# Two thirds of the gate projections by seven block products, in a stage of their own behind the attention

## The chip, the cores and the metric

The kernel runs on one core of a Trainium2 chip. The core has five engines with a queue of instructions each, worked off in order: TensorE (PE, matmuls), VectorE (DVE), ScalarE (ACT), GpSimd (POOL) and SyncE (SP), which here issues nearly all DMA transfers. The metric is the device time of one execution in microseconds (us), as the median of several runs.

## What is computed

One step of a hybrid encoder layer for 1152 tokens of width 1024, all in float32. The part that matters here is the gated merge of three branches:

```python
h = rmsnorm(x, p['g_pre1'])
y_ssm = y_ssm * jax.nn.sigmoid(y_ssm @ p['w_glu'] + p['b_glu'])
gates = jax.nn.sigmoid(h @ p['w_gate'] + p['b_gate']).reshape(bsz, L, N_BRANCH, D_MODEL)
merged = (gates[:, :, 0] * (y_ssm @ p['w_br_ssm'])
          + gates[:, :, 1] * (y_pool @ p['w_br_pool'])
          + gates[:, :, 2] * (y_mem @ p['w_br_mem']))
```

`w_gate` is 1024 x 3072: 24 blocks of 128 output columns, called gates 0 to 23 here (0 to 7 for the state-space branch, 8 to 15 for the pooling branch, 16 to 23 for the memory attention). Around the merge stand a state-space scan, a pooling branch, a small cross-attention, an output projection and a conv FFN, which the change leaves as they are.

## The kernel before, in words

Activations lie transposed: 128 features on the partitions, tokens along the row, in three chunks of 384 tokens. PE multiplies in a reduced float32 format (fp32r), so every operand is split into a high and a low part (`split`: ACT copies the high part, DVE subtracts to get the low one), and one product of a 128-row block is three matmuls, high x high, low x high, high x low (`mm3`, lines 101 to 107; the order prints the low part of h as hlo, of the weights as wlo). A gate of one chunk has 8 k-blocks, so 24 matmuls of 128x384, then DVE multiplies by the row norms (`scaled`, line 200), ACT takes the sigmoid (line 930), and the result, 192 KB, goes to a branch or is stored in the DRAM buffer `Dsg`.

The program runs through phase1 (norm, input projection, scan, attention, some gates), phase_g (branches and merge), phase_o (output projection), and the FFN. A scheduler orders each engine's instructions ahead of time; products without other ties are used as filler between the steps of the scan and the attention.

- **phase1** (line 864) puts 14 gates, 8 to 15 and 0 to 5, for all three chunks into `Dsg`, as filler beside scan and attention. The attention of the prompt (`attention`, lines 836 to 861) runs over two halves g and two head pairs hp; in each half a head's scores are four matmuls of 128x512, ACT takes the exponential, two matmuls sum over the memory (line 855), DVE takes a RECIPROCAL of 64x512 from PSUM and multiplies (lines 856, 857), and the result is stored to `Dmem` (line 858). Behind the first half stand the second part of the decode attention (64 matmuls of 128x32, line 769, that read four loads `cv`) and of the pooling branch.
- **phase_g** (line 992) loads the branch operands from `Dmem` and `Dpool` (`load_pair`, line 941; tile br), splits them (ohi, olo), and goes over f = 0 to 7 and the chunks. `branch` (line 979) computes gate 16 + f inline, 24 matmuls, beside 6 matmuls of the memory branch, then 6 of the pooling branch, whose gate is loaded from `Dsg` (tile sgl, 192 KB). Then `glu` (line 965) makes 48 matmuls a chunk, with a gate (number 6) between the chunks, and the last loop has the state-space branch, 12 matmuls per f and chunk, with gates from `Dsg` but the last (number 7), computed inline.

Apart from its weights a gate product in phase_g reads only SBUF: h stays there as hhi and hlo in all chunks.

## Time and profile before

| | us |
|---|---|
| median of 3 runs (lowest to highest) | 1556.09 (1555.48 to 1556.93) |
| profiled execution: its own time | 1553.49 |
| its span, first to last instruction | 1551.6 |
| PE busy | 1535.3 (99%) |
| DVE busy | 1018.7 (66%) |
| ACT busy | 583.5 (38%) |
| POOL busy | 442.1 (28%) |

The page's tables and the answers of the trace share a form: line of the code, engine, operation, output <- inputs, shape, count; then busy time in us, mean of one in ns, and the idle time before them with what ended it. In a timeline row the first number is the start and the second the duration; brackets hold the idle time before it and its releaser. Rows of a window give, for each engine, busy us and (x instructions), then the granted clock of PE (1.00 is full), the DMA share and GB/s. A row of waits gives the total, the number and the longest. Rows of transfers give the count, the size, and the median us from issue to landing. Neighbouring matmuls overlap in the records: their durations are longer than their distance.

### The profile page before, as it was taken

How to read it: one execution, taken by the hardware profiler on the slowest of the kernel's cores; microseconds unless marked ns; L12 is line 12 of the kernel's file. 1: busy time of each engine (PE TensorE's matmuls, PEld its weight loads, DVE VectorE, ACT ScalarE, POOL GpSimd, SP SyncE). 2: the span in 40 equal slices, each digit the busy share in tenths (PEclk: the TensorE clock that was granted, in tenths of full speed). 3: DMA queues.
4: the chain of work that ended last, by engine and by line, in shares of the span. 5: the costliest groups of instructions: out<-in, count | busy, mean ns of one | idle time of the engine just before them, and what ended most of it. 6: DMA issues, size and time to landing. Idle time of an engine off the chain costs nothing.

```text
span 1551.6 us, 22930 instructions
## 1 busy us (share of the span) xinstructions
PE 1535.3 (99%) x9016; PEld 1502.2 (97%) x9016; DVE 1018.7 (66%) x1606; ACT 583.5 (38%) x895; POOL 442.1 (28%) x425
## 2 busy tenths in 40 slices
PE   9999999999999999999999999999999999999997
PEld 8999998888999999999999999999999999999997
DVE  7956987556633354637587665665566569888876
ACT  8313445344311241435454333333343343333322
POOL 0000010000121243300025344344344311565545
PEclk9999999999999999999999999999999999999998
DMA  7533334422522235123413112212221243222224
GB/s 270 170 103 103 110 115 165 135 93 82 168 77 72 74 92 160 54 89 115 152 38 131 72 56 86 72 64 78 72 79 63 72 141 131 75 102 97 91 73 168
DMA packets 98029, 161.34 MB, mean 104 GB/s; under 512 B 23169, under 2 KB 68609, under 8 KB 97921
## 3 DMA queue, kind: packets, MB, share of 16 engines
q1 hardware_dynamic: 97488, 159.65, 31.4%
q8 instruction: 70, 1.15, 0.3%
q14 instruction: 39, 0.31, 0.1%
q10 hardware_dynamic: 432, 0.23, 0.1%
HBM read 117.43 MB, written 42.42 MB: 103 GB/s over the span
## 4 chain that ended last, share of the span: by engine, by line
PE 88%; DVE 6%; DMA 2%; ACT 2%; issue 1%; SPq 0%; POOL 0%; DVEq 0%; ACTq 0%; POOLq 0%
PE pc L107 16%; PE pc L103 16%; PE pc L106 16%; PE ps L103 11%; PE ps L106 11%; PE ps L107 11%; DMA Ts<-DG 1%; PE ps L855 1%; DMA DG<-gs 1%; ACT hhi L126 1%; DVE mg L1131 1%; PE ps L1078 0%; PE ps L769 0%; PE ps L821 0%; DVE Xs L604 0%
## 5 line engine op out<-in xcount | busy, mean ns | idle before, releaser
L103 PE MATMUL pc<-hhi,whi 128*128 128x384 f32 x760 | 257.1, 338 | 0.0
L107 PE MATMUL pc<-hhi,wlo 128*128 128x384 f32 x760 | 255.8, 337 | 0.3 <-DVE wlo L64 0.3
L106 PE MATMUL pc<-hlo,whi 128*128 128x384 f32 x760 | 256.1, 337 | 0.0
L63 ACT ACTIVATE whi<-rawt 128x1024 fp32r<-128x1024 f32 (+1 forms) x99 | 103.5, 1047 | 186.3 <-PE pc L106 78.3
L64 DVE TENSOR_TENSOR wlo<-rawt,whi 128x1024 fp32r<-128x1024 f32 (+1 forms) x99 | 122.5, 1239 | 54.6 <-ACT whi L63 54.2
L103 PEld LDWEIGHTS pc<-hhi,whi 128*128 128x128 f32 x760 | 142.7, 188 | 2.6 <-issue 1.1
L107 PEld LDWEIGHTS pc<-hhi,wlo 128*128 128x128 f32 x760 | 142.7, 188 | 2.3 <-issue 0.7
L106 PEld LDWEIGHTS pc<-hlo,whi 128*128 128x128 f32 x760 | 142.7, 188 | 2.0 <-issue 0.5
L200 DVE TENSOR_TENSOR sg<-pc,rb 128x384 f32<-128x384 f32 x95 | 52.3, 553 | 114.2 <-PE pc L107 112.8
L107 PE MATMUL pc<-h2hi,wlo 128*128 128x384 f32 x352 | 118.9, 338 | 0.0
L106 PE MATMUL pc<-h2lo,whi 128*128 128x384 f32 x352 | 118.3, 336 | 0.5 <-DVE h2lo L64 0.5
L103 PE MATMUL pc<-h2hi,whi 128*128 128x384 f32 x352 | 118.3, 336 | 0.0
L63 ACT ACTIVATE S<-S 128x512 fp32r<-128x512 f32 x80 | 50.2, 630 | 140.7 <-PE ps L107 86.9
L64 DVE TENSOR_TENSOR S<-S,S 128x512 fp32r<-128x512 f32 x80 | 68.7, 861 | 46.2 <-ACT S L63 44.2
L930 ACT ACTIVATE sg<-sg,vec 128x384 f32<-128x384 f32 x72 | 44.1, 612 | 141.4 <-DVE sg L200 112.8
L103 PE MATMUL ps<-bT,S 128*128 128x384 f32 x240 | 80.2, 334 | 0.0
L107 PE MATMUL ps<-bT,S 128*128 128x384 f32 x240 | 80.2, 334 | 0.0
L106 PE MATMUL ps<-bT,S 128*128 128x384 f32 x240 | 80.2, 334 | 0.0
L1017 POOL TENSOR_TENSOR mg<-mg,sgl 128x384 f32<-128x384 f32 x24 | 29.1, 1213 | 165.4 <-DVE sgl L1015 162.0
L63 ACT ACTIVATE dhi<-dwr 128x1024 fp32r<-128x1024 f32 x38 | 39.6, 1057 | 84.4 <-PE pc L106 49.2
L106 PEld LDWEIGHTS pc<-h2lo,whi 128*128 128x128 f32 x352 | 66.0, 187 | 0.8 <-DVE h2lo L64 0.8
L107 PEld LDWEIGHTS pc<-h2hi,wlo 128*128 128x128 f32 x352 | 66.1, 188 | 0.0
(449 smaller groups left out, 4225.9 us busy)
## 6 DMA issues: line engine op xcount, KB each, us to landing
rawt<-in_w_up SPq DMA_DIRECT2D x44, 512.0 KB, 3.4
Dact<-t SPq DMA_DIRECT2D x22, 576.0 KB, 3.6
rawt<-in_w_gate SPq DMA_DIRECT2D x24, 512.0 KB, 3.6
dwr<-in_w_down SPq DMA_DIRECT2D x22, 512.0 KB, 3.4
Dsg<-sg SPq DMA_DIRECT2D x45, 192.0 KB, 1.8
sgl<-Dsg SPq DMA_DIRECT2D x45, 192.0 KB, 2.4
dBr<-Dact SPq DMA_DIRECT2D x8, 768.0 KB, 5.0
xT<-in_xT SPq DMA_DIRECT2D x12, 384.0 KB, 7.6
```

Of the source, the lines that this page charges most:

```text
L63: a = nc.scalar.activation(hi, src, AF.Copy)
L64: return a, (eng or nc.vector).tensor_sub(lo, src, hi)
L103: i = nc.tensor.matmul(out, whi, xhi, start=start, stop=False)
L106: nc.tensor.matmul(out, whi, xlo, start=False, stop=False)
L107: nc.tensor.matmul(out, wlo, xhi, start=False, stop=stop)
L126: a = nc.scalar.activation(hi[:, k, :], x[:, k, :], AF.Copy, scale=g)
L200: self.nc.vector.tensor_mul(sg, b, self.rb[:, c, :])
L855: nc.tensor.matmul(o, va[:, m, 2 * hp + e, :], pT[:, m, :], start=m == 0, stop=m == 1)
L930: self.nc.scalar.activation(sg, sg, AF.Sigmoid, bias=self.vec[:, V_BGATE + m:V_BGATE + m + 1])
L1017: nc.gpsimd.tensor_add(m, m, sp)
L1131: V.scalar_tensor_tensor(oT[:, f, :], oT[:, f, :], self.vec[:, V_GPRE2 + f:V_GPRE2 + f + 1], rb, op0=OP.mult, op1=OP.mult)
```

## The change

Gates 8 to 15 stay in phase1 for all chunks. Gates 16 to 23 and 0 to 7 are taken in 8 pairs of neighbours. For chunk 2 each is computed as before, in phase1. For chunks 0 and 1 a pair is a 2 x 2 block product: two gates' weights, each in two halves of k (a11, a12, a21, a22), times two chunks of h, each in two halves of k (b11, b21, b12, b22). It is computed by seven products of sums of blocks, each with 4 k-blocks (12 matmuls), where there were eight (the form of Strassen's scheme due to Winograd).

- `blocks` loads xT of chunks 0 and 1 once more (8 transfers of 384 KB, issued behind the first store of the attention, `att_half`), scales them to h on DVE (16 instructions of 128x384, line 964 of the new file), and forms the sums with 5 subtractions of 128x1536 and 7 splits of 128x1536 (tiles bB11, bB21, bB22, bT1 to bT4).
- Still in phase1, the two products with a11 and a12 (on bB11 and bB21) use the split weights of the even gate that chunk 2 uses. Their sum is the even gate of chunk 0; the first is kept (tile u).
- `phase_s`, a new stage between phase1 and phase_g, loads the raw weights of a pair again (2 x 512 KB), forms four sums on DVE (128x512), splits five operands, runs five products in the order 6, 5, 7, 3, 4, and adds the results on DVE, POOL and ACT into the other three gates of the pair, which are stored to `Dsg`.
- `branch` no longer computes a gate: all 24 come from `Dsg`, the pool of the loaded gates has 6 buffers for 3, and the gate between the glu chunks is gone.

```diff
-        self.Dsg = D.tile([9 + NSG, 3, 128, 384], F32, name="Dsg")
+        self.Dsg = D.tile([24, 3, 128, 384], F32, name="Dsg")
...
+            for m in range(8, 16):
+                gates(m, range(3))
+            self.blocks()
+
+            for m in self.strassen_gates()[1::2]:
+                gates(m, (2,))
+            self.su = []
+            for m in self.strassen_gates()[0::2]:
+                gw = gates(m, (2,))
+                self.su.append(su.tile([128, 384], F32, tag="su", name="u"))
+                for n, ks in (("B11", slice(0, 4)), ("B21", slice(4, 8))):
+                    b = self.block(self.pc(), [w[:, ks] for w in gw], n)
...
+    def blocks(self):
+        V = self.nc.vector
+        lo, up = slice(0, 4), slice(4, 8)
+        with self.tc.issue_after(self.att_half.ins):
+            h = [self.h_load(c) for c in range(2)]
+        for c in range(2):
+            for k in range(8):
+                V.scalar_tensor_tensor(h[c][:, k, :], h[c][:, k, :], self.vec[:, V_GPRE1 + k:V_GPRE1 + k + 1],
+                                       self.rb[:, c, :], op0=OP.mult, op1=OP.mult)
...
+        op("B11", h0[:, lo])
+        op("B21", h0[:, up])
...
+                V.tensor_add(s1, a21, a22)
+                V.tensor_sub(s2, s1, a11)
...
+            nxt = weights(0)
+            for j in range(8):
+                cur, nxt = nxt, weights(j + 1) if j < 7 else None
+                for p in (6, 5, 7, 3, 4):
+                    prod(cur, p)
...
-        if gw is None:
-            sg = self.load_gate(P, 8 + f, c)
-        else:
-            sg = self.gate(P, 8 * g + f, self.proj(gw, c, 8, *self.hx()), c)
+        sg = self.load_gate(P, 8 * g + f, c)
...
-            for c in range(3):
-                os.append(self.glu(P, w, c))
-                nc.sync.dma_start(self.Dsg[8 + NSG, c], self.gate(P, NSG, self.proj(gw, c, 8, *self.hx()), c))
-            os = self.opx(os)
+            os = self.opx([self.glu(P, w, c) for c in range(3)])
...
+        k.phase_s()
+        k.rbs.close()
         k.phase_g()
```

Up to the attention the engines' orders are the same. Three places behind that are shown. The first is DVE's order in the attention of the prompt, from the third of eight reciprocals; yt is the attention's output, wlo a gate weight's low part. Before:

```order
574 L856 RECIPROCAL yt<-ps 64x512
575 L857 TENSOR_TENSOR yt<-ps,yt 64x512
576 L200 TENSOR_TENSOR sg<-pc,rb 128x384
577 L64 TENSOR_TENSOR wlo<-rawt,whi 128x1024
578 L856 RECIPROCAL yt<-ps 64x512
579 L857 TENSOR_TENSOR yt<-ps,yt 64x512
580 L200 TENSOR_TENSOR sg<-pc,rb 128x384
```

And of the changed kernel, from the same reciprocal to the low part of B21 (bB_3484 is B11, bB_3487 is B21):

```order
580 L855 RECIPROCAL yt<-ps 64x512
581 L964 SCALAR_TENSOR_TENSOR xT<-xT,vec,rb 128x384 x3
582 L199 TENSOR_TENSOR sg<-pc,rb 128x384
583 L964 SCALAR_TENSOR_TENSOR xT<-xT,vec,rb 128x384 x3
584 L856 TENSOR_TENSOR yt<-ps,yt 64x512
585 L964 SCALAR_TENSOR_TENSOR xT<-xT,vec,rb 128x384 x4
586 L855 RECIPROCAL yt<-ps 64x512
587 L964 SCALAR_TENSOR_TENSOR xT<-xT,vec,rb 128x384 x4
588 L63 TENSOR_TENSOR bB_3484<-xT,bB_3484 128x1536
589 L964 SCALAR_TENSOR_TENSOR xT<-xT,vec,rb 128x384 x2
590 L63 TENSOR_TENSOR bB_3487<-xT,bB_3487 128x1536
```

Fourteen of the sixteen scalings and a second reciprocal now stand between the third reciprocal and the low part of B11. PE's order at the same place, from the fourth head's sums (at) over the decode attention (PT, cv) on. Before:

```order
1727 L855 MATMUL ps<-at_2255 128x512
1728 L769 MATMUL ps<-PT,cv 128x32 x2
1729 L855 MATMUL ps<-at_2255 128x512
1730 L769 MATMUL ps<-PT,cv 128x32 x14
1731 L107 MATMUL pc<-hhi,wlo 128x384
1732 L103 MATMUL pc<-hhi,whi 128x384
```

And of the changed kernel:

```order
1724 L854 MATMUL ps<-at_2258 128x512
1725 L768 MATMUL ps<-PT,cv 128x32 x8
1726 L854 MATMUL ps<-at_2258 128x512
1727 L768 MATMUL ps<-PT,cv 128x32 x8
1728 L102 MATMUL pc<-bB_3484,whi 128x384
1729 L768 MATMUL ps<-PT,cv 128x32 x16
1730 L105 MATMUL pc<-bB_3484,whi 128x384
1731 L106 MATMUL pc<-bB_3484,wlo 128x384
```

Where a gate on hhi stood, the first product on B11 stands now. The second place is the beginning of phase_g on PE. Before, the first branch product (ohi, olo) is mixed with a gate (hhi, hlo):

```order
2041 L103 MATMUL ps<-ohi,whi 128x384
2042 L103 MATMUL pc<-hhi,whi 128x384
2043 L106 MATMUL pc<-hlo,whi 128x384
2044 L107 MATMUL pc<-hhi,wlo 128x384
2045 L103 MATMUL pc<-hhi,whi 128x384
2046 L106 MATMUL pc<-hlo,whi 128x384
2047 L107 MATMUL pc<-hhi,wlo 128x384
2048 L106 MATMUL ps<-olo,whi 128x384
```

And of the changed kernel, from the last block product (bT4) on; ohi_5223 and ohi_5227 are the first memory operand, ohi_5233 belongs to the first pooling operand:

```order
L106 MATMUL pc_5185<-bT4_3507,A22_5033 128x384
L102 MATMUL ps_5286<-ohi_5223,whi_5217 128x384
L105 MATMUL ps_5286<-olo_5224,whi_5217 128x384
L106 MATMUL ps_5286<-ohi_5223,wlo_5218 128x384
L102 MATMUL ps_5286<-ohi_5227,whi_5217 128x384
L102 MATMUL ps_5294<-ohi_5233,whi_5217 128x384
L105 MATMUL ps_5286<-olo_5228,whi_5217 128x384
L106 MATMUL ps_5286<-ohi_5227,wlo_5218 128x384
```

Only branch products follow the last block product. SP's transfers there, before, with the last store of the attention (yt), the last store of a gate (sg), branch operands (br) and loaded gates (sgl):

```order
L858 DMA Dmem_84<-yt_2674 128x4x128
L925 DMA Dsg_98<-sg_4009 128x384
L941 DMA br_4063<-Dmem_84 128x2x384
L935 DMA sgl_4149<-Dsg_98 128x384
L935 DMA sgl_4196<-Dsg_98 128x384
L935 DMA sgl_4243<-Dsg_98 128x384
L941 DMA br_4073<-Dpool_85 128x2x384
L941 DMA br_4083<-Dmem_84 128x2x384
L941 DMA br_4093<-Dpool_85 128x2x384
```

And of the changed kernel, where x of phase_o comes in ahead, and the last gate's store is sg_5198:

```order
L1039 DMA Dsg_98<-sg_5181 128x384
L1230 DMA x_7015<-in_xT 128x768
L1230 DMA x_7039<-in_xT 128x768
L1073 DMA sgl_5284<-Dsg_98 128x384
L1039 DMA Dsg_98<-sg_5198 128x384
L1073 DMA sgl_5301<-Dsg_98 128x384
L1073 DMA sgl_5305<-Dsg_98 128x384
L1073 DMA sgl_5322<-Dsg_98 128x384
L1073 DMA sgl_5326<-Dsg_98 128x384
L1073 DMA sgl_5343<-Dsg_98 128x384
L1079 DMA br_5251<-Dpool_85 128x2x384
L1079 DMA br_5261<-Dmem_84 128x2x384
```

The load of br_5271 follows; three loaded gates stood ahead of the last three operands before, six now, and two loads of x. The third place is glu on PE, from the end of chunk 0's last product (pc_5402 before, pc_5908 now). Before, the gate (hhi_155) follows:

```order
L103 MATMUL pc_5402<-ohi_5332,whi_5302 128x384
L106 MATMUL pc_5402<-olo_5333,whi_5302 128x384
L107 MATMUL pc_5402<-ohi_5332,wlo_5303 128x384
L103 MATMUL pc_5424<-hhi_155,whi_5308 128x384
L106 MATMUL pc_5424<-hlo_156,whi_5308 128x384
```

Now chunk 1's first operand (ohi_5935) is read at once:

```order
L102 MATMUL pc_5908<-ohi_5838,whi_5814 128x384
L105 MATMUL pc_5908<-olo_5839,whi_5814 128x384
L106 MATMUL pc_5908<-ohi_5838,wlo_5815 128x384
L102 MATMUL pc_5956<-ohi_5935,whi_5808 128x384
L102 MATMUL pc_5978<-ohi_5935,whi_5808 128x384
```

More of the change, by code (lines that the diff above doesn't have):

```diff
@@ L19 @@
 EPS = 1e-6
-NSG = 6
 V_GPRE1, V_GPRE2, V_GMEM, V_BGATE, V_BGLU = 0, 8, 16, 24, 48
@@ L857, in attention @@
                     nc.vector.tensor_mul(yf[es], o[es], yf[es])
-                nc.sync.dma_start(self.Dmem[hp].rearrange("p (j k) -> p j k", j=8)[:, gs, 0:128], yt)
+                i = nc.sync.dma_start(self.Dmem[hp].rearrange("p (j k) -> p j k", j=8)[:, gs, 0:128], yt)
+                if g == hp == 0:
+                    self.att_half = i
             if g == 0:
@@ L917, in phase1, with gates @@
             nc.sync.dma_start(self.O["pool"], self.pout)
-            for f in range(8 + NSG):
-                m = 8 + f if f < 8 else f - 8
+            def gates(m, chunks):
                 with tc.high_priority():
                     gw = self.load_w(self.I["w_gate"][m])
-                for c in range(3):
+                for c in chunks:
                     b = self.proj(gw, c, 8, *self.hx())
                     with tc.high_priority():
-                        nc.sync.dma_start(self.Dsg[f, c], self.gate(P, m, b, c))
+                        nc.sync.dma_start(self.Dsg[m, c], self.gate(P, m, b, c))
+                return gw
@@ new lines, in phase1 @@
+            for m in range(8, 16):
[9 more added lines that the diff above has]
+                    b = self.block(self.pc(), [w[:, ks] for w in gw], n)
+                    with tc.high_priority():
+                        if n == "B11":
+                            nc.scalar.activation(self.su[-1], b, AF.Copy)
+                        else:
+                            sg = P.tile([128, 384], F32, tag="sg", name="sg")
+                            nc.vector.tensor_add(sg, self.su[-1], b)
+                            nc.scalar.activation(sg, sg, AF.Sigmoid, bias=self.vec[:, V_BGATE + m:V_BGATE + m + 1])
+                            nc.sync.dma_start(self.Dsg[m, 0], sg)
@@ new lines, in strassen_gates, with op @@
+    @staticmethod
+    def strassen_gates():
+        return [*range(16, 24), *range(8)]
+    def blocks(self):
[7 more added lines that the diff above has]
+                                       self.rb[:, c, :], op0=OP.mult, op1=OP.mult)
+        h0, h1 = h
+        self.B = {}
+        def op(name, src):
+            t = self.mtile([128, 2, 4, 384], F32R, "b" + name)
+            self.B[name] = t[:, 0], t[:, 1]
+            self.split(t[:, 0], t[:, 1], src)
+        op("B11", h0[:, lo])
+        op("B21", h0[:, up])
+        V.tensor_sub(h0[:, up], h0[:, up], h0[:, lo])
+        op("B22", h1[:, up])
+        V.tensor_sub(h0[:, lo], h1[:, lo], h0[:, lo])
+        V.tensor_sub(h1[:, lo], h1[:, up], h1[:, lo])
+        V.tensor_sub(h1[:, up], h1[:, up], h0[:, lo])
+        V.tensor_sub(h0[:, up], h0[:, up], h1[:, lo])
+        op("T1", h0[:, lo])
+        op("T3", h1[:, lo])
+        op("T2", h1[:, up])
+        op("T4", h0[:, up])
@@ L1011, in phase_g @@
                 for c in range(3):
-                    self.branch(P, gw, bw, 2, 4 * (f % 2), 2, f, c, om)
+                    self.branch(P, bw, 2, 4 * (f % 2), 2, f, c, om)
                     b = self.proj(bw, c, 2, *op, wk=4 * (f % 2) + 2, bank=self.sm())
-                    sp = self.load_gate(P, f, c)
+                    sp = self.load_gate(P, 8 + f, c)
                     nc.vector.tensor_mul(sp, b, sp)
```

83 lines of the change are left out of this document (67 added, 16 removed).

## The prediction

> **What bounds the kernel now.** I read the page first, its busy line and its chain of waits.
>
> ```profile
> PE 1535.3 (99%) x9016; PEld 1502.2 (97%) x9016; DVE 1018.7 (66%) x1606; ACT 583.5 (38%) x895; POOL 442.1 (28%) x425
> PE 88%; DVE 6%; DMA 2%; ACT 2%; issue 1%; SPq 0%; POOL 0%; DVEq 0%; ACTq 0%; POOLq 0%
> ```
>
> PE is busy in 99% of the span and makes 88% of the chain that ends last, so a matmul taken out is time taken out, as long as nothing puts a hole in its place. Then the waits of PE alone, the longest first, and windows of the stage that the change rebuilds:
>
> ```profile
> PE ps L268 <- DVE pr L395: 1.4, 1, 1.4
> PE ps L96 <- ACT diag L94: 1.3, 1, 1.3
> ...
> 436.00:456.00 20.00, 20.00 (x118) 20.00 (x117) 8.52 (x14) 3.97 (x6) 3.95 (x3) 1.00 0.26 83
> 456.00:476.00 20.00, 20.00 (x117) 20.00 (x116) 7.34 (x12) 3.87 (x5) 3.78 (x4) 1.00 0.23 68
> ```
>
> No wait of PE is longer than 1.4 us. In the gate stage (436 to 476) PE is full while VectorE (DVE) works 8.5 and 7.3 of 20 us: whatever DVE, ScalarE (ACT) and the DMAs need there is hidden under the gate matmuls. That cover is what the change takes away in some places.
>
> **What one matmul costs.** The windows hold 235 matmuls of 128x384 in 40 us, one each 0.170 us, and 117 in 20 us are 0.171; a few matmuls more or less at the edges make it 0.17 to 0.174.
>
> ```profile
> L103 PE MATMUL pc<-hhi,whi 128*128 128x384 f32 x760 | 257.1, 338 | 0.0
> ```
>
> The 338 ns of this row are start to end of overlapping matmuls; 117 of them would fill 39.5 us, and the window has 20. I take 0.1725 us. The change saves, for each of 8 pairs of gates and chunks 0 and 1, 96 matmuls against 7 products of 12, that is 84: 8 x 12 = 96 matmuls, **16.6 us**. (With 338 ns it would be 32.4 us; the windows exclude that.) All other PE work moves without changing its number.
>
> **The price, first place: the first product of block B11.** In the second half of the attention DVE now carries the rescaling of h: from the third reciprocal to the split of B11 stand the reciprocal itself, 14 STTs of 128x384, one gate evacuation, one multiply, a further reciprocal, and the split. PE's first low-part matmul of B11 stands directly behind 32 small matmuls of the decode attention.
>
> ```profile
> 332.49 3.36 DVE L856 RECIPROCAL yt<-ps 64x512 f32<-64x512 f32 x1 [2.04 <-PE ps L855]
> ...
> L1131 DVE SCALAR_TENSOR_TENSOR mg<-mg,vec,ps 128x384 f32<-128x384 f32 x24 | 12.9, 608 | 12.1 <-PE ps L96 12.1
> L200 DVE TENSOR_TENSOR sg<-pc,rb 128x384 f32<-128x384 f32 x95 | 52.3, 553 | 114.2 <-PE pc L107 112.8 <-ACT rb L177 0.8
> L857 DVE TENSOR_TENSOR yt<-ps,yt 64x512 f32<-64x512 f32 x8 | 5.5, 688 | 0.2
> L64 DVE TENSOR_TENSOR bB<-mg,bB 128x1536 fp32r<-128x1536 f32 x4 | 6.9, 1751 | 4.7 <-ACT bB L63 4.7
> ...
> 331.44 1.02 PE L855 MATMUL ps<-at 128*128 128x512 f32 x2
> 336.59 1.02 PE L855 MATMUL ps<-at 128*128 128x512 f32 x2
> 337.45 0.53 PE L769 MATMUL ps<-PT,cv 128*128 128x32 f32 x4
> 337.81 1.10 PE L855 MATMUL ps<-at 128*128 128x512 f32 x2
> 338.75 3.21 PE L769 MATMUL ps<-PT,cv 128*128 128x32 f32 x28
> ```
>
> DVE: 3.36 + 14 x 0.608 + 0.55 + 0.69 + 3.36 + 1.75 = 18.2 us (17.2 if STTs follow each other at 0.54). PE, from the end of the same L855 pair (332.5): five 128x512 matmuls at 512/384 of 0.1725, 1.2, five gate matmuls 0.9, then what stands here from 336.59 to 341.96, 5.4, and one B11 matmul 0.2: 7.7 to 8. It then waits **9.7 us** (9.2 to 10.5); behind it in PE's queue stand only gates and products that are not to be had earlier, since the queue is in order. The reload of h does not set this: it is issued behind the first store of the attention, about 2 us ahead of the third reciprocal (DVE's idle time in its row), and
>
> ```profile
> xT<-in_xT SPq DMA_DIRECT2D x12, 384.0 KB, 7.6
> ```
>
> its like land 7.6 us after issue, while the last tile needed is read some 15 us after that reciprocal starts. On SP the eight loads stand ahead of two loads of the decode attention (cv) and delay them, and the 16 small matmuls that read them, by up to 8 x 0.58 us of issue time (row of three sgl loads, below): inside the same 9.7 us. Until phase_s DVE has the remaining STTs, 5 subtractions, 6 splits of 128x1536 and the pool branch beside it, and PE's chunk-2 gates need its evacuations. Following both queues with the rows' durations, PE meets DVE late once more, before the third even gate, by **1.2 us** (0.9 to 2), and then no more: the last operand that phase_s needs first (T2) is ready 2 us early.
>
> **A slower clock behind that hole.** The end of the program shows what PE's clock does when PE has little to do, and an early gap what it does not do.
>
> ```profile
> 1538.00:1540.00 2.00, 2.00 (x10) 2.00 (x9) 0.00 (x0) 0.59 (x2) 1.37 (x2) 0.68 0.52 196
> 1540.00:1542.00 2.00, 2.00 (x5) 0.73 (x3) 0.00 (x0) 0.40 (x2) 0.00 (x0) 0.50 0.00 1
> 1542.00:1544.00 2.00, 0.10 (x1) 0.00 (x0) 1.86 (x4) 0.00 (x0) 0.65 (x1) 0.97 0.02 4
> ...
> 29.89 0.91 PE L96 MATMUL ps<-diag,ones 128*128 128x384 f32 x2 [1.30 <-ACT diag L94]
> ```
>
> The granted clock falls to 0.50 and is back after 1.28 + 2.0 + 0.12 = 3.4 us; after a wait of 1.3 us PE's clock stayed at 1.00. A hole of 7 us or more (9.7 with small interruptions) should bring one such stretch, 3.4 us at half speed: **1.7 us**, bounds 0 and, if a second place does it too, 3.4. [...]
>
> **Second place: from phase_s into phase_g.** Before, a gate's projection from SBUF ran while the branch operands were loaded and split:
>
> ```profile
> 404.78 0.53 ACT L63 ACTIVATE ohi<-br 128x384 fp32r<-128x384 f32 x1 [2.11 <-DMA Dmem<-yt]
> ...
> 408.00 0.53 ACT L63 ACTIVATE ohi<-br 128x384 fp32r<-128x384 f32 x1 [1.36 <-DMA br<-Dmem]
> ...
> 411.99 1.98 ACT L63 ACTIVATE ohi<-br 128x384 fp32r<-128x384 f32 x4 [2.54 <-DMA br<-Dpool]
> 414.26 0.94 ACT L63 ACTIVATE ohi<-br 128x384 fp32r<-128x384 f32 x2 [0.30 <-DMA br<-Dpool]
> ...
> 405.22 1.74 SPq L935 DMA_DIRECT2D sgl<-Dsg  x3
> ...
> L930 ACT ACTIVATE sg<-sg,vec 128x384 f32<-128x384 f32 x72 | 44.1, 612 | 141.4 <-DVE sg L200 112.8
> Dsg<-sg SPq DMA_DIRECT2D x45, 192.0 KB, 1.8
> br<-Dpool SPq DMA_DIRECT2D x3, 384.0 KB, 4.2
> ```
>
> Those splits took from 404.8 to 415.2. Now the first branch products follow the last block product (its end is T) with no gate between. The third operand's split reuses memory that the last gate store must have left: DVE add 0.55, sigmoid 0.61, store 1.8, with two 384 KB loads of x for phase_o just ahead in SP's queue: T + 3.5 to 4.2, then splits at 0.53 each. SP issues at 0.33 to 0.58 us per transfer (the row of three in 1.74); twelve stand ahead of and with the last three operand loads, so the last is issued at T + 5.1, lands at T + 9.3 and is split by T + 10.4. PE has 42 matmuls, 7.3 us, up to there and one k-step behind: a loss of about **4.5 us** (3.5 to 7).
>
> **Third place: from glu's chunk 0 to chunk 1.** Here the rows show the wait itself:
>
> ```profile
> 557.01 0.33 PE L107 MATMUL pc<-ohi,wlo 128*128 128x384 f32 x1
> ...
> 557.44 0.58 ACT L972 ACTIVATE sg<-pc,vec 128x384 f32<-128x384 f32 x1
> 558.72 0.53 ACT L63 ACTIVATE ohi<-sg 128x384 fp32r<-128x384 f32 x1 [0.69 <-DVE sg L975]
> 559.15 1.75 ACT L63 ACTIVATE ohi<-br 128x384 fp32r<-128x384 f32 x4
> ...
> 561.35 0.68 PE L103 MATMUL pc<-ohi,whi 128*128 128x384 f32 x3
> ```
>
> Glu's last product of chunk 0 starts at 557.01; chunk 1's first split is done at about 559.65. The 24 gate matmuls that ran until 561.35 are gone, and PE waits from 557.2 to 559.7: **2.5 us**. Between chunks 1 and 2 twelve branch matmuls (2.1 us) remain as cover: 0.3. Together 2.8 (2 to 4).
>
> **What stays hidden.** In phase_s a pair costs PE 60 x 0.1725 = 10.4 us; DVE has 9 operations of 128x512 and 4 evacuations.
>
> ```profile
> L64 DVE TENSOR_TENSOR S<-S,S 128x512 fp32r<-128x512 f32 x80 | 68.7, 861 | 46.2 <-ACT S L63 44.2
> L64 DVE TENSOR_TENSOR wlo<-rawt,whi 128x512 fp32r<-128x512 f32 x2 | 1.4, 688 | 4.8 <-ACT whi L63 4.8
> ```
>
> At 688 ns that is 9 x 0.688 + 4 x 0.553 = 8.4 us, at 861 ns 10.0: below 10.4 either way. [...] In the branches each chunk now loads two gates of 192 KB per 12 matmuls (2.1 us), 190 GB/s, with six buffers instead of three; for that and small waits I add 0.5 us (0 to 3). Nothing behind phase_g changes.
>
> **The sum.** Saved 16.6; lost 9.7 + 1.2 + 1.7 + 4.5 + 2.8 + 0.5 = 20.4 us: 3.8 us slower. The profiled execution took 1553.5 us, so 1557.3; the median of the runs shown, 1556.1, is 2.6 us above it, and I predict **1560 us** for the median. About 0.2% (3.1 us) is what a measurement of this kernel can tell from no change.
>
> **Rivals.**
> - *As summed, or worse by its upper bounds* (1559.2 to 1567): the B11 hole, phase_g's start and glu together outweigh the saving. For it: DVE's queue is in order, and its 18 us are rows. 0.46.
> - *The waits just eat the saving.* With all at the lower ends and no slow clock, 9.2 + 0.9 + 3.5 + 2 = 15.6: 1 us faster, 1555; up to 1559. 0.28.
> - *Faster: only the hole in the attention is real.* If the loads for phase_g land under the last block products and glu's wait is filled, as today no wait of PE passes 1.4 us, the loss is 9.7 + 1.2 = 10.9: 5.7 us faster, 1550.4, and without the 1.2 us 1549. It decides if PE goes on in phase_g within 1 us of T. Against it: a split waits for a store that cannot start before T. 0.22.
> - *Slower: DVE becomes the bound of phase_s.* It needs DVE 5% above the 10.0 us a pair; at 10% (11.0) each pair loses 0.6 us, 8 pairs 4.8, on top of the sum: 1565, and with a second stretch at half clock 1567. The windows' 8.5 of 20 us speak against a DVE that is nearly full, the 861 ns row for it. 0.04.
>
> That the saving fails to appear in PE's count isn't open: 96 matmuls are gone.
>
> **Range and chances.** Lower ends and part of the faster case give 1549, upper ends 1568; the likeliest case's own range is 1557 to 1567. Faster by over 0.2%: 0.22; within: 0.28; slower: 0.46 + 0.04 = 0.50.
>
> **What would show it.** In the profile after: a wait of PE on DVE bB of 7 to 10 us near 345 to 352 with the granted clock below 1 behind it; ohi and olo as releasers of 3 to 6 us of PE at phase_g's start; 2.5 us on ohi in glu; no wait inside phase_s. PE's waits adding up to less than 14 us would prove the forecast wrong, as would a cadence in the block products other than 0.17 us.

## The result and the profile after

| | before | after |
|---|---|---|
| median of 4 runs each (lowest to highest), us | 1555.78 (1555.43 to 1556.93) | 1565.29 (1563.88 to 1565.91) |
| profiled execution: its time / its span, us | 1553.49 / 1551.6 | 1565.68 / 1563.9 |

The ratio is 1.0056 (95% interval 1.0044 to 1.0069): 0.56% slower, 8.7 us on 1555.8 (the medians lie 9.5 us apart). The forecast was 1560, in a range of 1549 to 1568. The two profiled executions differ by 12.3 us of span, of which 11.1 have come about when the first matmul of phase_o starts (648.7 us before, 659.8 after), and the account below is made up to there.

First the busy line and the chain of waits on the page after:

```profile
PE 1531.3 (98%) x8920; PEld 1495.1 (96%) x8920; DVE 1101.5 (70%) x1714; ACT 625.6 (40%) x958; POOL 459.7 (29%) x441
PE 85%; DVE 7%; DMA 4%; ACT 2%; issue 2%; SPq 0%; POOL 0%; DVEq 0%; ACTq 0%; POOLq 0%
```

The 96 matmuls are gone (8920 for 9016), and PE is busy 4 us less, not 16.6: busy time counts slow matmuls too (from 590 to 600, below, PE is busy for 10.00 us with 48 matmuls at a clock of 0.80, where full windows have 59 or 60). PE's share of the chain has gone from 88 to 85%. Then the longest waits of PE:

```profile
PE ps L102 <- ACT ohi L62: 7.6, 4, 3.7
PE pc L102 <- ACT ohi L62: 3.6, 1, 3.6
PE ps L768 <- DMA cv<-in_cv: 2.5, 1, 2.5
```

Before, no wait was longer than 1.4 us. The second row is glu between chunks 0 and 1 (pc); the first (ps) is the start of phase_g with 1.82, 3.67 and 0.56 us, and one more wait of 1.51 us behind glu. All waits of PE add up to 22.8 us, 6.8 before; less than 14 would have proved the forecast wrong. The wait on bB of 7 to 10 us that the prediction named is not among them. Windows of the three places (columns as before: PE, its weight loads, DVE, ACT, POOL, granted clock, DMA share, GB/s):

```profile
344.00:346.00 2.00, 0.92 (x5) 0.92 (x5) 1.97 (x2) 0.77 (x1) 0.00 (x0) 0.72 0.83 334
350.00:352.00 2.00, 2.00 (x11) 2.00 (x11) 2.00 (x2) 0.00 (x0) 0.12 (x1) 0.50 0.90 251
354.00:356.00 2.00, 2.00 (x10) 2.00 (x10) 1.89 (x5) 0.42 (x1) 0.00 (x0) 0.72 0.07 24
...
370.00:380.00 10.00, 10.00 (x59) 10.00 (x58) 9.85 (x16) 3.19 (x5) 0.00 (x0) 1.00 0.29 103
...
510.00:520.00 10.00, 6.80 (x37) 5.89 (x35) 2.13 (x4) 3.17 (x6) 1.98 (x2) 0.95 0.44 143
520.00:530.00 10.00, 7.00 (x28) 6.28 (x29) 6.57 (x13) 4.57 (x10) 1.29 (x1) 0.71 0.88 297
530.00:540.00 10.00, 8.68 (x49) 8.04 (x48) 6.72 (x12) 3.18 (x3) 4.02 (x4) 1.00 0.94 314
...
580.00:590.00 10.00, 6.42 (x34) 6.10 (x33) 8.63 (x15) 5.90 (x12) 6.88 (x7) 0.86 0.17 49
590.00:600.00 10.00, 10.00 (x48) 10.00 (x48) 4.89 (x6) 3.10 (x5) 3.98 (x4) 0.80 0.38 111
...
610.00:620.00 10.00, 8.49 (x48) 7.90 (x47) 9.01 (x14) 6.12 (x11) 2.79 (x3) 1.00 0.55 175
```

Read the (x) behind PE: a full window of 10 us has 59 or 60 matmuls. The second place (510 to 540) lacks 23 + 32 + 11 = 66, at 0.17 us each 11.2 us; the third (580 to 600 and 610 to 620) lacks 26 + 12 + 12 = 50, 8.5 us. The window before them (370 to 380) is full, as are all from 440 to 510, the whole of phase_s. And the clock is below 1.00 at all three places, where the prediction counted one slow stretch.

The rows behind these windows, from the timelines of DVE, PE, ACT and SP (start, duration, then the instruction, and in brackets the idle time before it; SPq is SP's queue of transfers):

```profile
334.36 3.36 DVE L855 RECIPROCAL yt<-ps 64x512 f32<-64x512 f32 x1 [2.63 <-PE ps L854]
...
349.88 1.84 DVE L63 TENSOR_TENSOR bB<-xT,bB 128x1536 fp32r<-128x1536 f32 x1
...
342.11 0.45 PE L102 MATMUL pc<-bB,whi 128*128 128x384 f32 x1 [0.54 <-ACT bB L62]
345.08 7.03 PE L768 MATMUL ps<-PT,cv 128*128 128x32 f32 x32 [2.52 <-DMA cv<-in_cv]
351.93 0.67 PE L105 MATMUL pc<-bB,whi 128*128 128x384 f32 x1
...
517.38 0.45 PE L102 MATMUL ps<-ohi,whi 128*128 128x384 f32 x1 [1.82 <-ACT ohi L62]
522.44 0.69 PE L102 MATMUL ps<-ohi,whi 128*128 128x384 f32 x1 [3.67 <-ACT ohi L62]
...
521.87 1.76 ACT L62 ACTIVATE ohi<-br 128x384 fp32r<-128x384 f32 x4 [4.13 <-DMA Dsg<-sg]
...
515.59 0.81 SPq L1230 DMA_DIRECT2D x<-in_xT  x2
...
516.96 0.38 SPq L1039 DMA_DIRECT2D Dsg<-sg  x1
...
588.54 1.65 PE L102 MATMUL pc<-ohi,whi 128*128 128x384 f32 x4 [3.58 <-ACT ohi L62]
...
613.66 0.62 PE L102 MATMUL ps<-ohi,whi 128*128 128x384 f32 x2 [1.51 <-ACT ohi L62]
```

At the first place DVE needs 17.4 us from the start of the third reciprocal (334.36) to the end of B11's split (349.88 + 1.84 = 351.72), in the prediction 17.2 to 18.2, and PE's first low-part product follows at 351.93. But PE did not idle until then: from 345.08 it worked off 32 small matmuls of the decode attention in 7.03 us, 0.22 us each, where the same 32 took 3.65 us before, 0.114 each:

```profile
345.90 3.65 PE L769 MATMUL ps<-PT,cv 128*128 128x32 f32 x32
```

It had waited 2.52 us for their cv load, and the clock fell to 0.50 as they began (0.72 in 344 to 346, then 0.50). Two chains end here within 0.2 us of each other. At the second place the last gate store, issued at 516.96 behind the two loads of x, has not landed before about 521.8, 4.9 us later (median of its kind 1.8); ACT waits 4.13 us for it and PE 3.67 us for ACT. At the third place the wait is 3.58 us, where the prediction had 2.5: ACT starts the splits of chunk 1 3.4 us after glu's last product of chunk 0 (584.62 to 587.98), in the kernel before 2.1. The last row is a fourth wait: behind glu's chunk 2 the state-space branch waits for the split of that chunk's own result, where a gate followed before.

The account up to phase_o: 16.6 saved. Phase_g has 720 matmuls, which at the cadence of phase_s (480 from 432.0 to 515.2, 0.1737 us each) are 125.1 us; from the last block product to the first matmul of phase_o it took 144.6. So the second and third place cost 19.5 us together, as by the windows (11.2 + 8.5). The first place is then 11.1 + 16.6 - 19.5, about 8 us. Its rows say the same: waits of 0.5 and 2.5 us, 3.4 us by which the small matmuls ran slower, and 1.5 us for ten matmuls on B11 at 0.32 us.

### The profile page after: what moved, and what is told of

It reads as the page before. It is cut to its first block, busy times and chain, and to the rows that moved or that the text cites. A ratio compares the mean times of both kernels' runs of the same rounds, so it can differ in the third digit from the quotient of the medians.

```text
span 1563.9 us, 23115 instructions
## 1 busy us (share of the span) xinstructions
PE 1531.3 (98%) x8920; PEld 1495.1 (96%) x8920; DVE 1101.5 (70%) x1714; ACT 625.6 (40%) x958; POOL 459.7 (29%) x441
## 4 chain that ended last, share of the span: by engine, by line
PE 85%; DVE 7%; DMA 4%; ACT 2%; issue 2%; SPq 0%; POOL 0%; DVEq 0%; ACTq 0%; POOLq 0%
PE pc L102 15%; PE pc L106 15%; PE pc L105 15%; PE ps L102 12%; PE ps L105 12%; PE ps L106 12%; DMA Ts<-DG 1%; PE ps L854 1%; DMA DG<-gs 1%; ACT hhi L125 1%; PE ps L768 1%; DVE mg L1254 1%; PE ps L1201 0%; PE ps L820 0%; DVE Xs L603 0%
## 5 line engine op out<-in xcount | busy, mean ns | idle before, releaser
L102 PE MATMUL pc<-hhi,whi 128*128 128x384 f32 x504 | 171.1, 339 | 0.0
L105 PE MATMUL pc<-hlo,whi 128*128 128x384 f32 x504 | 170.9, 339 | 0.0
L106 PE MATMUL pc<-hhi,wlo 128*128 128x384 f32 x504 | 170.0, 338 | 0.3 <-DVE wlo L63 0.3
L63 DVE TENSOR_TENSOR S<-S,S 128x512 fp32r<-128x512 f32 x112 | 91.2, 820 | 50.4 <-ACT S L62 48.2
L102 PE MATMUL ps<-bT,S 128*128 128x384 f32 x304 | 101.5, 334 | 0.0
L105 PE MATMUL ps<-bT,S 128*128 128x384 f32 x304 | 101.5, 334 | 0.0
L106 PE MATMUL ps<-bT,S 128*128 128x384 f32 x304 | 101.5, 334 | 0.0
L106 PEld LDWEIGHTS pc<-hhi,wlo 128*128 128x128 f32 x504 | 94.6, 188 | 2.3 <-DVE wlo L63 0.6
L105 PEld LDWEIGHTS pc<-hlo,whi 128*128 128x128 f32 x504 | 94.7, 188 | 1.9 <-issue 0.2
L102 PEld LDWEIGHTS pc<-hhi,whi 128*128 128x128 f32 x504 | 94.7, 188 | 1.8 <-issue 0.7
L102 PE MATMUL ps<-ohi,whi 128*128 128x384 f32 x192 | 65.1, 342 | 8.9 <-ACT ohi L62 7.6
L102 PEld LDWEIGHTS pc<-h2hi,whi 128*128 128x128 f32 x352 | 66.0, 188 | 0.0
```

What stands on the lines that cost most here:

```text
L63: return a, (eng or nc.vector).tensor_sub(lo, src, hi)
L102: i = nc.tensor.matmul(out, whi, xhi, start=start, stop=False)
L105: nc.tensor.matmul(out, whi, xlo, start=False, stop=False)
L106: nc.tensor.matmul(out, wlo, xhi, start=False, stop=stop)
```

## The experiments

Twelve kernels ran, each beside the kernel before on the same chip. The kernel before had medians of 1555.09, 1555.68 and 1555.97 us on the three chips, so gains below are differences of the ratios, in us of 1556; those under 2 us are within the intervals. The last three columns are read off the timelines of PE: the start of the first matmul of phase_s, of the last one before the branches, and of the first of phase_o. The first shows what the first place cost, the third all of it; they come from a single execution each.

| kernel | median, us | ratio to before (95%) | phase_s starts | phase_s ends | phase_o starts |
|---|---|---|---|---|---|
| before | 1555.78 | | | | 648.7 |
| after | 1565.29 | 1.0056 (1.0044 to 1.0069) | 432.0 | 515.2 | 659.8 |
| e1_plain | 1571.91 | 1.0103 (1.0087 to 1.0118) | | | 667.1 |
| e2_early_h | 1561.83 | 1.0046 (1.0034 to 1.0059) | 425.2 | 513.6 | 656.2 |
| e3_fill | 1562.15 | 1.0046 (1.0033 to 1.0058) | 435.2 | | 658.2 |
| e4_noreuse | 1562.72 | 1.0049 (1.0037 to 1.0062) | 433.8 | 517.0 | 658.5 |
| e5_b11 | 1564.77 | 1.0057 (1.0043 to 1.0070) | 434.3 | 518.7 | 661.2 |
| e6_fill6 | 1556.29 | 1.0005 (0.9996 to 1.0014) | 433.7 | | 651.8 |
| e7_both | 1557.20 | 1.0011 (1.0001 to 1.0020) | 432.0 | | 648.4 |
| e8_dummy | 1564.87 | 1.0059 (1.0046 to 1.0071) | 432.8 | 516.0 | 658.9 |
| e9_u3 | 1562.67 | 1.0052 (1.0040 to 1.0065) | 431.7 | 514.9 | 657.5 |
| e10_u3_b11 | 1560.48 | 1.0037 (1.0025 to 1.0049) | 427.2 | 512.2 | 655.1 |
| e11_best | 1549.58 | 0.9960 (0.9947 to 0.9973) | 432.0 | | 644.9 |
| e12_noreuse6 | 1559.83 | 1.0024 (1.0013 to 1.0036) | 433.6 | 516.6 | 655.5 |

The theory at the start was the prediction's own, three places that lost their cover; the rivals are named with each run.

### e1_plain: the move without the saving

```diff
-            for m in range(8, 16):
+            for m in (*range(8, 24), *range(8)):
                 gates(m, range(3))
-            self.blocks()
...
-        k.phase_s()
```

> The move without the saving: all 24 gates are computed plainly for the three chunks in the gate stage and stored, no block products and no new stage; the branches read every gate from DRAM, as in the changed kernel. Theory (phase_g lost its cover, and that alone costs what the profile shows at the second and third place, about 10 and 8 us, half clock included): before + 12 to + 20 us, 1568 to 1576, with waits of PE on ohi at the start of phase_g and between glu's chunks and cadence 0.32 us behind them. Rival (the loss is made by the block products and their stage; reading gates back is free): within 4 us of before, 1552 to 1560. If only the numbers of the prediction were right (4.5 + 2.8): before + 7 us, 1563.

Ratio 1.0103, 16.0 us slower than before, and 18.4 us later at phase_o. The windows of its phase_g start and glu, and the row of ACT's wait for the last gate store:

```profile
520.00:530.00 10.00, 8.23 (x47) 7.76 (x45) 1.69 (x4) 2.65 (x5) 0.00 (x0) 1.00 0.11 39
530.00:540.00 10.00, 9.62 (x36) 8.64 (x36) 8.00 (x17) 4.73 (x12) 1.01 (x1) 0.66 0.72 225
...
590.00:600.00 10.00, 6.91 (x41) 6.59 (x40) 9.76 (x14) 5.32 (x11) 6.95 (x7) 1.00 0.05 11
600.00:610.00 10.00, 9.15 (x49) 7.99 (x47) 4.73 (x9) 4.59 (x9) 2.04 (x2) 1.00 0.43 134
...
531.14 1.76 ACT L62 ACTIVATE ohi<-br 128x384 fp32r<-128x384 f32 x4 [1.12 <-DMA Dsg<-sg]
```

The same two holes, at the same points of the program, in a kernel without one block product. Not all of the 18.4 us belong to them: from the last gate matmul (527.6) to phase_o (667.1) are 139.5 us, 14.4 more than the 720 matmuls need. About 3 of the other 4 us lie ahead of the attention, which the edit does not touch, and the rest is a slow clock in it (last section). So taking the gates out of phase_g costs 14 to 16 us by itself, nearly what the block products save (16.6). That is the larger part of the loss, and the numbers of the prediction (7 us) are excluded. The changed kernel loses 5 us more than this one in phase_g: here no loads of x stand ahead of the last store, ACT waits 1.12 us for it instead of 4.13, and the windows from 520 to 550 lack 7 us instead of 11.

### e2_early_h: h rescaled before the attention

```diff
-        with self.tc.issue_after(self.att_half.ins):
-            h = [self.h_load(c) for c in range(2)]
+        h = [self.h_load(c) for c in range(2)]
```

> The changed kernel, with h of chunks 0 and 1 reloaded and rescaled as early as its memory allows, instead of behind the first store of the attention. Theory (the first place is DVE's queue, rescaling and reciprocals ahead of the split of B11): PE's hole of 8 to 9 us near 343 to 352 and the half clock behind it go, 9 to 10 us, 1554 to 1557; the two other places stay. Rival (the hole comes from the attention's own chain, or the STTs just push the reciprocals and PE's softmax products back by as much): 1562 to 1566, with PE waits on DVE yt or on Exp in the attention instead.

The hole and the slow clock at 344 to 355 are gone (the clock is 1.00 there), and phase_s starts 6.8 us earlier. It ends only 1.6 us earlier: the scheduler now stretches the second half of the attention, its last reciprocal ends at 424.9, and behind it DVE is late with the split of T2, with which phase_s begins:

```profile
428.85 0.58 PE L105 MATMUL pc<-bT,S 128*128 128x384 f32 x1 [3.31 <-DVE bT L63]
```

A wait of 3.3 us and another stretch at half clock (428.98 to 432.40) give 5.2 of the 6.8 us back. The forecast of 9 to 10 us failed (1.6 by the ratio); 1561.8 is where the rival had it, though the late operand is T2 and not yt.

### e5_b11: only what B11 needs ahead of its split

```diff
+        with self.tc.high_priority():
+            scale(0, range(4))
+            first = op("B11", h0[:, lo])
+            with self.tc.issue_after(first[1].ins):
+                scale(0, range(4, 8))
+            second = op("B21", h0[:, up])
+        with self.tc.issue_after(second[1].ins):
+            scale(1, range(8))
```

> The changed kernel, with B11 first: the four rescalings that block B11 needs, its split, then four more and the split of B21, and the eight of chunk 1 behind that; ten of the fourteen rescalings that stood ahead of B11's split on DVE now stand behind it, the fourth reciprocal still ahead. Theory (the first place is DVE's order and nothing else): B11's low part is ready 10 x 0.54 = 5.4 us earlier, PE's hole falls from 8.4 to about 3 us and the half clock behind it (1.5 us) goes with it; B21's split is ready before PE has done the 19 gate matmuls ahead of it: 5 to 7 us faster than the changed kernel, 1558 to 1560. Rival (PE is held there by the decode attention's loads of cv, or the stall only goes to the next operand, as it did in part when h was loaded early): under 2.5 us gained, 1563 to 1565.

No gain (1.0057). The split is done at 346.5 instead of 351.7, as forecast, and PE does not profit:

```profile
344.86 3.62 PE L768 MATMUL ps<-PT,cv 128*128 128x32 f32 x16 [2.12 <-DMA cv<-in_cv]
348.30 0.67 PE L105 MATMUL pc<-bB,whi 128*128 128x384 f32 x1
...
351.96 3.46 PE L768 MATMUL ps<-PT,cv 128*128 128x32 f32 x16
```

The wait for cv, and the 16 small matmuls at half clock behind it, hold the first low-part product until 348.30. Then the other 16 stand between B11 and the next products, and the clock does not come back before 360.5:

```profile
360.00:362.00 2.00, 2.00 (x12) 2.00 (x11) 0.67 (x1) 0.00 (x0) 0.00 (x0) 0.87 0.00 0
```

In the changed kernel it was back at 355.1. The theory that DVE's order alone makes the first place fell here, and the theory of two chains replaced it.

### e9_u3 and e10_u3_b11: the two chains apart and together

```diff
-"U": pool("p1u", 2)
+"U": pool("p1u", 3)
```

This is all of e9_u3: the third cv load no longer waits for a buffer until the loads of h fill the DMAs (410 and 376 GB/s, a share of 1.04 and 1.02, in 340 to 342 and 342 to 344 of the changed kernel; there it landed 6.1 us after its issue at 338.96). e10_u3_b11 has e5's edit as well.

> The changed kernel with three instead of two buffers for the tiles of the decode attention's cv loads, so that only the last of four loads, and not two, is still to come when the eight loads of h fill the DMAs. DVE's order is as in the changed kernel. Theory (two chains end at about the same time at the first place: DVE's, with the split of B11 done at 351.7 us, and PE's own, with 32 small matmuls at half clock behind a cv load that lands late, done at 352.0): taking away the second alone gains at most 2 us, 1563 to 1566, and the profile now shows PE waiting for DVE's bB. Rival (the late cv load and the half clock set the first place by themselves): 5 us or more, 1557 to 1560.

> Three cv buffers and B11 first, together: both chains of the first place shortened. Theory of two chains: neither edit gains more than 2 us alone, both together gain 5 to 8 us, 1557 to 1560, with the granted clock at 1.00 between 340 and 362 us or low for 4 us at most. Rival (a third thing holds PE there, or DVE is late again before phase_s): under 3 us, 1562 to 1565.

In e9_u3 the small matmuls are through early, and now the profile shows a wait on DVE's bB, as the prediction had described it, though of 2.12 us; the split is done at 350.34:

```profile
346.41 1.87 PE L768 MATMUL ps<-PT,cv 128*128 128x32 f32 x16
...
350.39 0.69 PE L105 MATMUL pc<-bB,whi 128*128 128x384 f32 x1 [2.12 <-DVE bB L63]
```

Phase_s starts 0.3 us earlier than in the changed kernel, and the ratio is 1.0052 for 1.0056: taking away the second chain alone gains nothing that can be told, like e5_b11 with the first. Both together let it start 4.8 us earlier. Of these 1.8 are lost at once to the next late operand:

```profile
429.02 0.44 PE L105 MATMUL pc<-bT,S 128*128 128x384 f32 x1 [1.52 <-DVE bT L63]
```

What stays is 3.0 us at the end of phase_s, and 1.0037 for 1.0056. In e10_u3_b11 PE has neither wait at the first place, for cv or for bB, so both chains are shown; the size, 5 to 8 us, was not reached, and the rival (DVE late again) was partly right. Nor can the 4.8 us be put down to the two edits: e11_best, below, has the same orders of PE there and starts phase_s at 432.0, like the changed kernel, because its clock stays low for longer (13.6 us for 3.4).

### e4_noreuse and e12_noreuse6: the memory of the branch operands

Both keep the pools of phase_s open over phase_g, so that the operands no longer lie where the last gate tiles lie; the order of PE stays. e4_noreuse paid for the memory with 4 instead of 6 buffers for loaded gates, e12_noreuse6 puts weight blocks into free tiles and keeps 6.

```diff
-        with ExitStack() as ctx:
+        ctx = self.ss = ExitStack()
...
         k.phase_s()
         k.rbs.close()
         k.phase_g()
+        k.ss.close()
```

> As the run with held-back products, with the same memory and buffers, but all five products of the last pair stand ahead of the first branch as in the changed kernel: only the reuse of the last gate tiles' memory by the branch operands is gone. Theory (second place is the landing of the last gate store, which the first operand split waits for): the splits go on under the last block products and 7 to 11 us are gained, 1554 to 1558, third place unchanged. Rival (the queue of SP or the loads' bandwidth set the second place): under 3 us gained, 1562 to 1566.

> As the held-back run with full buffers, but all five products of the last pair ahead of the first branch: against the changed kernel only the memory of the branch operands differs (it is no longer that of the last gate tiles). Theory (the second place is the wait of the first operand split for the last gate store, and what it drags behind it): 7 to 10 us gained, 1555 to 1558, the third place as before. Rival (without other matmuls the operands are late all the same, by SP's queue and the loads): under 4 us, 1561 to 1565.

In both the first branch product follows phase_s within 0.2 us, where it took 2.2, and the wait of 3.67 us is gone, so the shared memory, and with it the landing of the last store, made that hole. But e4_noreuse gained 1.1 us and e12_noreuse6 5.0, not 7 to 11. In e4_noreuse the third place, which was to stay, got worse; why is not shown:

```profile
590.24 1.65 PE L102 MATMUL pc<-ohi,whi 128*128 128x384 f32 x4 [6.86 <-ACT ohi L62]
```

In e12_noreuse6 a new wait stands 17 us after the end of phase_s, for a gate that has to come back from DRAM (DVE waits 5.03 us for it), with its own slow clock behind it:

```profile
530.00:540.00 10.00, 7.45 (x33) 6.81 (x32) 4.66 (x8) 1.06 (x1) 4.18 (x4) 0.83 0.66 216
...
533.59 0.44 PE L102 MATMUL ps<-ohi,whi 128*128 128x384 f32 x1 [2.27 <-DVE sgl L1157]
```

From 510 to 520 the DMAs moved 386 GB/s at a share of 1.04: with the operands in time, the reload of two gates per 12 matmuls is next. The second place is a store's landing first and the DMAs second; the rival was partly right. No run moved the two loads of x by themselves.

### e3_fill and e6_fill6: matmuls held back as cover

The five products of the last pair of gates (needed last, gates 6 and 7) are split up: two ahead of the first branch, two between glu's chunks 0 and 1, one between chunks 1 and 2. Both keep the pools open like the runs above.

```diff
+            self.tail = [lambda p=p: prod(cur, p) for p in (6, 5, 7, 3, 4)]
...
+            for t in self.tail[:2]:
+                t()
...
-            os = self.opx([self.glu(P, w, c) for c in range(3)])
+            os = []
+            for c in range(3):
+                os.append(self.glu(P, w, c))
+                for t in self.tail[2 + 2 * c:4 + 2 * c]:
+                    t()
+            os = self.opx(os)
```

> The changed kernel, with the five products of the last pair of gates held back: two stand between phase_s and the first branch, two between glu's chunks 0 and 1, one between chunks 1 and 2; the operands' memory is then not that of the last gate tiles (the stage has 6 instead of 8 result buffers and 2 instead of 4 for A22, the branches 4 instead of 6 gate buffers). Theory (both places are chains that need only a few us of other matmuls): second place from about 10 us to under 2, third from about 8 to under 3, so 13 to 17 us faster than the changed kernel: 1548 to 1552. Rival (the places are bound by DMA bandwidth, near 390 GB/s there, or by DVE): the waits only move behind the filler, under 5 us gained, 1560 to 1565.

> The run with held-back products again, without what it had taken away: six gate buffers in the branches, eight result buffers, and the held-back weight blocks (S3, S4, A22) in their own memory, not in the ring of weight tiles that the glu weights need. Theory (that run's gain was eaten by these two shortages: waits on mg and sgl of about 7 us, on whi and wlo with a half clock of about 6): both go, 1548 to 1552. Rival (the branches are bound by the reload of the gates from DRAM, whatever the buffers): the waits on mg and sgl stay and less than 6 us are gained over the 1562 of that run, 1556 to 1562.

e3_fill gained 1.6 us, far from 13 to 17. The waits on ohi are nearly gone, but new ones have come in their place:

```profile
PE ps L102 <- DVE mg L1127: 2.2, 3, 0.9
PE pc L106 <- DVE wlo L63: 2.0, 2, 1.7
PE ps L102 <- DVE sgl L1154: 1.9, 2, 1.3
```

The reading was that four gate buffers are too few and that the held-back weight blocks took the ring that the glu weights need. With both mended at once e6_fill6 is 8 us faster than the changed kernel, 1.0005 to before. From 510 to 630 its windows lack 65 matmuls, e3_fill's 95, the changed kernel's 119. That is at the lower end of the rival's range (1556 to 1562), not in the theory's: mg is waited for 0.2 us instead of 2.2, but one wait of 1.9 us for whi and one of 2.6 us for sgl stay.

### e8_dummy: the half clock by itself

```diff
+                if c == 0:
+                    b = self.pc()[:, 0:384]
+                    wd = w[0][0]
+                    for _ in range(18):
+                        i = nc.tensor.matmul(b, wd[:, 0, :], wd[:, 0:3, :].rearrange("p k n -> p (k n)"), start=True, stop=True)
+                        tc.keep_in_program_order(i)
```

> The changed kernel with 18 matmuls without use, 3.1 us, between the last product of glu's chunk 0 and the first of chunk 1, where PE waits 3.6 us; nothing waits for them. Theory (the half clock behind that wait costs about 3 us and is set by PE being idle there): PE starts chunk 1 as late as before, but its cadence behind it is 0.17 instead of 0.32 us, 2.5 to 3 us faster: 1562 to 1563. Rival (the low clock comes from elsewhere, or the matmuls delay chunk 1): no faster than the changed kernel, 1565 or more.

PE starts chunk 1 at 588.7, as late as before (588.5), and now at full clock. The window of the changed kernel, then that of this one:

```profile
588.00:592.00 4.00, 3.46 (x11) 3.46 (x12) 3.89 (x5) 1.73 (x5) 2.78 (x3) 0.50 0.28 68
```

```profile
588.00:592.00 4.00, 3.49 (x21) 3.26 (x20) 3.88 (x6) 1.92 (x5) 2.59 (x3) 1.00 0.22 51
```

Between 588 and 596 PE makes 46 matmuls for 30, 2.7 us of work. That the clock falls there because PE is idle is shown: 0.50 in the first window, 1.00 in the second, with 18 matmuls in the place of the wait. The time is nevertheless the same (1.0059): at 597 to 602 PE now waits for weights (wlo, 0.64 us) and small things, from phase_s's end to phase_o it is 142.9 us for 144.6, and 1.7 us are within the intervals of the two ratios. So the theory was right on the clock, and the rival on the time: PE's lost work is not worth its full price where it then runs into operands that are late anyway.

### e7_both and e11_best: all that helped

e7_both is e6_fill6 with B11 first; e11_best has three cv buffers as well, and loads the first weights of the state-space branch ahead of glu.

```diff
             w = [self.load_w(self.I["w_glu"][i]) for i in range(2)]
+            bw0 = self.load_w(self.I["w_brs"][0])
...
-                bw = self.load_w(self.I["w_brs"][f0 // 2])
+                bw = bw0 if f0 == 0 else self.load_w(self.I["w_brs"][f0 // 2])
```

> B11 first and the held-back products with full buffers, together. Theory (first place and phase_g's places are independent): the gains add, 1565 less 6 less 13 to 17: 1542 to 1547, faster than the kernel before by 0.5 to 0.8%. Rival (they share a bound, DVE or the DMAs): 1550 or more.

> All that helped: three cv buffers, B11 first, the last pair's products held back with full buffers, and the first weights of the state-space branch loaded ahead of glu. Theory (first place and phase_g's places add): 1556.3 of the held-back run less 5 to 8 for the first place and up to 2 for the weights: 1546 to 1551, faster than the kernel before by 0.3 to 0.6%. Rival (the gains don't add, as with B11 first in the run of both): 1554 to 1557, the same as before.

e7_both is where e6_fill6 is, far from its 1542 to 1547: B11 first gains nothing, as without the held-back products. e11_best comes out at 0.9960 (0.9947 to 0.9973), 6.2 us faster than the kernel before and 15 faster than the changed one: the theory's range, but not by its sum. Its phase_s starts as late as in the changed kernel, so nothing comes from the first place; from there to phase_o it needs 212.9 us, e6_fill6 218.1 and the changed kernel 227.8. The wait for whi ahead of the state-space branch (1.9 us in e6_fill6, 1.8 in e7_both) is gone with the weights there early, and the order around it is another; no run has this edit alone. Windows of glu and behind it:

```profile
580.00:590.00 10.00, 10.00 (x59) 10.00 (x58) 6.41 (x12) 6.59 (x13) 2.46 (x3) 1.00 0.17 59
590.00:600.00 10.00, 10.00 (x59) 10.00 (x59) 4.74 (x7) 4.83 (x8) 3.69 (x5) 1.00 0.88 283
600.00:610.00 10.00, 9.12 (x53) 8.80 (x52) 9.65 (x15) 3.05 (x6) 5.04 (x4) 1.00 0.65 204
```

The third place is gone but for 9 matmuls, 1.5 us; from 510 to 630 the windows lack 23 in all. The first place of this run says something else. From 312 us to phase_s PE has the same matmuls in the same order as in e10_u3_b11, without a wait, and up to 338 us it runs 0.09 us behind it. The clock is then low for 13.6 us (343.0 to 356.6) instead of 3.4 (343.7 to 347.1), and behind that this run is 4.9 us late, up to phase_s (432.0 for 427.2).

## Why the prediction was right and where it was wrong

**The sign** came out by the mechanism that the likeliest case gave: places that lose their cover cost more than 96 matmuls save. 1565.3 is 5 us above the forecast, and that it is not further off is luck in part: up to phase_o about 28 us were lost where the sum had 20.4, 4 to 5 less than forecast at the first place and 12 more in phase_g.

**The saving, 16.6 us**: 96 matmuls are gone, and the block products run at 0.17 us in full windows. Right. It does not show in PE's busy time, which counts slow matmuls as work: about 9 us of it are the half clock's (3.4 + 1.5 at the first place, 1.7 and 2.8 at the others).

**The first place: 12.6 us forecast (9.7 + 1.2 + 1.7), about 8 measured.** DVE's chain took 17.4 us, forecast 17.2 to 18.2, and the distance on PE came out too: 342.11 to 351.93 between the first two matmuls on B11, 9.7 us besides the matmul itself. The step that failed here is that all of it was counted as a hole. In it stand 32 small matmuls, 3.65 us of work at full clock, so 6 us were lost there and 0.5 just ahead. And DVE's chain is one of two: the cv loads, which the prediction put "inside the same 9.7 us", delay the small matmuls into the slow clock, and these end at the same time (e5, e9, e10). The second meeting before the third even gate, 1.2 us, did not come: the windows from 360 to 380 are full. The slow clock took 3.4 us of the small matmuls' time, hidden under DVE's chain, and 1.5 us of ten matmuls on B11 at 0.32 us; 1.7 was forecast.

**The second place: 4.5 us forecast (3.5 to 7), 11 measured.** The step that failed here is the landing of the last store. The prediction gave it the median of 1.8 us and saw the two loads of x ahead of it only as time to issue; it took 4.9 us, while the DMAs moved 369 GB/s (518 to 520); in e1_plain, with no loads of x ahead of it, the wait for it is 1.12 us. Behind it came a slow clock, which the prediction had counted for the first place alone (0.71 granted in 520 to 530), and the gates' reload, for which 0.5 us stood in the sum (e12_noreuse6). The 4.5 was not fully worked out either: its last split at T + 10.4 less 7.3 us of matmuls leaves 3.1.

**The third place: 2.8 us forecast (2 to 4), 8 measured.** Of this 3.7 are the gap between chunks 0 and 1 (2.5 forecast; ACT comes to the splits of chunk 1 later than before, as above) and 2.8 the slow clock behind it, which e8_dummy shows. Between chunks 1 and 2, where 0.3 was forecast, PE is full (600 to 610). The last 1.7 are the gap behind chunk 2 (613.66), a place that lost its gate as well and that the prediction did not count.

**Phase_s** has no wait inside, DVE at 7.5 to 9.7 of 10 us: right, and the rival of a DVE bound is out. The faster rival (only the attention's hole is real) is out by e1_plain. "The waits just eat the saving" describes e6_fill6, where phase_g's waits are mostly covered.

**The clock** was counted as one stretch of 3.4 us. It was low for 10.2, 6.8 and 6.8 us at the three places (worked out below), of which only the time with matmuls that others wait for is lost. The prediction had a second stretch, 1.7 us more, only as its upper bound; the sum with it is nearer, and still short. That it takes a hole of 7 us or more was the author's estimate: the clock fell behind waits of 1.8 us too (e1_plain, last section).

**Still open**: what the first place costs without the slow clock. With the same orders of PE it differs by 4.9 us between e10_u3_b11 and e11_best through the clock alone, as much as the two chains seemed to be worth. In e10_u3_b11 the next bound is DVE's split of T2; whether it is the only one, no run shows.

## What to carry to other kernels

Work that looks like mere arithmetic may be the cover of something else: before you remove or move matmuls, list what each stretch of them hides, and price the bare chain with landing times under load, not with medians (4.9 us here for 1.8). The hole of 3.58 us behind glu's chunk 0 cost 2.8 us again in slow clock, so work that is needed anyway, held back for the seams, can win back much of what the move lost (60 matmuls, 8 us in e6_fill6). Where undoing one cause gains nothing, look for a second chain that ends at the same time before you drop the theory.
